# A new instruction order for a hybrid decoder layer, one sum for half of the first scale, and a last norm sum on VectorE

## The chip, the core and the metric

The kernel runs on one core of one Trainium2 chip. The metric is device time in microseconds (us) of one execution; the lower the better. A core has five engines that run side by side, each through its own list of instructions in order: PE (TensorE: matmuls), ACT (ScalarE), DVE (VectorE), POOL (GpSimd), and SP (SyncE), which here only issues DMA transfers. An instruction that has to wait for another engine or for a transfer holds up all that stand behind it on its own engine.

## The reference

One decoder layer on `x` of 1024 tokens by 1024 columns in fp32, with a vector `c` that gives shifts, scales and gates:

```python
c_act = silu(c)
mod = c_act @ w_mod + b_mod
sh1, sc1, g1, sh2, sc2, g2 = split(mod, 6)
h = rms_norm(x, norm_mix_w) * (1.0 + sc1) + sh1
proj = h @ w_in
...
h_lru = rg_lru(xr, r_pre, i_pre, lam)
out_lru = rms_norm(h_lru * gelu(y_lru), lru_norm_w)
...
out_gdn = rms_norm(o, gdn_norm_w) * silu(z)
x = x + g1 * (concatenate([out_lru, out_gdn]) @ w_out)
h = rms_norm(x, norm_mlp_w) * (1.0 + sc2) + sh2
x = x + g2 * (square(relu(h @ w_up)) @ w_down)
return rms_norm(x, final_norm_w)
```

`rg_lru` is a recurrent group of 512 channels: two gates from small block matmuls and sigmoids, then a scan over the tokens, h = a * h + b. `o` comes from the gated delta rule over four heads of 128, in chunks. The norm of `out_lru` is over all 512 channels of a token.

## The kernel before

**Numbers.** A matmul of fp32 quality is made of three matmuls on parts: each operand is split into a high part (`h`, rounded to the faster type fp32r by a cast on ACT) and a low part (`l`, the difference, on DVE or POOL), and `mm3` adds high x high, high x low and low x high in one PSUM bank. Small matmuls that need no such split (sums over partitions against `ones`, transposes) are plain fp32, each in two passes on PE. So behind nearly every matmul stand a load, a cast and a subtraction.

**Stages, in order.** (1) The start: `x` is loaded in eight tiles (`x0` to `x7`), each row is normed, transposed on PE, and scaled by A1 = (1 + sc1) * norm weight into `hT` (parts `hh`, `hl`). sc1 is a product of the vector `c_act` with a 1024x1024 part of `w_mod`. Its first 256 columns come from `scale0` (L755), one 128-column piece each, and its next 256 from `scale1(1)`, by matmuls against `cz`. The last 512 come from `scale1(2)` (L766): the weights `sc1_w20` to `sc1_w23` (512 KB each) are multiplied by `c_act` and added up over the eight row blocks k, and PE sums over partitions against `ones` (the fp32 matmuls `sc_c<-ones,sc_acc`, one per 128 columns). Before, there are two such sums, for k = 0 to 3 and k = 4 to 7; PE adds them, eight matmuls in all. Key weights `wk0` to `wk3` are loaded meanwhile, `wk0` in halves; `splitk` (L712) makes `wkh` and `wkl`, and the first matmuls are those of the four key heads (`k_p`). (2) The other projections, the delta rule's chunk inverse and its four heads' chain (`ch`, `cho`), with ACT's and DVE's steps between the matmuls. (3) The recurrent group, `lru` (L1229), four tiles of 128 channels (ct = 0 to 3). Each tile has its gates by a group of six fp32r matmuls on 64 of the 128 partitions each (`gate`), tanh on ACT (`ta`, `ti`), an exponential (`aa`), a square, a square root, then on DVE the product with the scan (`xr`) and with gelu(y) (`ly_st`). `ly_st` is stored to DRAM (`lrud`), ACT squares it (`lsq`), and L1265 adds the square to `msum` on POOL, for tiles 1 to 3 (tile 0's square is `msum` itself). (4) `rows8` (L1307) makes the norm: PE sums `msum` over partitions (`lrus`), DVE transposes, POOL takes the power -0.5 (`rsqrt8`, L529), and the row goes by DRAM (`lnd`) to be read back on all partitions (`lrus_b`). `catload` (L1333) loads `ly_st` back (`lcm0` to `lcm3`), multiplies it by `lrus_b` on DVE, and `hsplit` (L1327) makes `lch` and `lcl`. (5) The output projection: weights `wo0` to `wo7` (`wout`, L1344: parts `woh` on ACT, `wol` on DVE). The delta rule's half, `wg` (parts `gch`, `gcl` of the loaded `gcm`), can run before the recurrent norm is there. `wl` needs it (`finish`, L1394); four of its sixteen sums begin with the matmuls of `gch`. `gated` (L1374) adds the residual: `x <- wg,g,xT` on DVE, with the residual loaded as eight tiles `xT` (`residual`, L1366). (6) The second norm, once for each half of the tokens (`norm2`, L1414): `n2` sums on PE, POOL's power (`n_r`), and a transpose on PE (`n2b`). (7) The MLP: up-projection in sixteen blocks and down-projection, both by a scheme with seven products in place of eight (operands `U`, `wu`, `upx`, `upy`, `upz`; left operands `L` and right operands `R`, sums `dn`). Product at = 5 has as its right operands R0_5 to R7_5, and at = 7 R0_7 to R7_7: two loads each, a subtraction on POOL (`right`, L1673), a cast on ACT and a subtraction on DVE. (8) Residual, final norm, output tiles `fin`.

**What sets the order.** Nothing runs in the order of the source. Every instruction is recorded, and `emit` (L320 to L333) issues the records in the order of a list of numbers, `ORDER`, unpacked from the packed text `_ORDER` (L115 and on). It is a permutation of the 8013 records. `_SLOTS` says, for each tile, which buffer of its pool it gets: 46 buffers of 4 KB per partition (and 6 late ones), 8 PSUM banks. So the tables set for each engine what stands behind what; for SP they set in which order the transfers are issued, and which earlier user a load has to wait for. Nearly all DMAs are issued by SP. For that reason nearly all rows of the profile carry L333, the line that issues a record (or L459, that of a group of matmuls), and are told apart by their tiles; numbers at the end of a tile's name are left out in the profile.

Of the kernel before, what the change touches and what calls it, by code (L numbers as in the profile page):

```python
# [106 lines left out]
def dram_box(ap):  # L107
# [12 lines left out]
    'cuBSW<*M>pV)hgv~a=|gSHZ*}B7yt+XjF!lp&CO7mhb0x}Y9U^nMGb1w<B03R{s!q|W5+|4OKz@#0V4S0@CEBAVg>~c$E!R4cP0XAfA5`M5#`3KeX0!~lGn77@9ee)L'  # L120
    '^!Tx!e8@_SR5o|)XnhN>R%68L+8NB$BYrjIE-Sc4%*SbNX@V!Fv)1CA>!?r2I7u`cZ78aP&Pl0Zu3`Hm)-y%EVs){SQ`XvIrjW7rnx4nLcsaoTft<u|h6ouM%~g5zaV'
    'f=`7UI8)(olcVn=(s#XbWQTq<LtKOu@&kbOmc`tKUn4PGF>79;tDBeqP#YE3U{Sz11BnCR?$&x%YJ|`B-yE7Z9J0XeZ(M2l^OZKEayaV3k8zUp47Wymx~~H&YbZR2<A'
    'aDI4*`6dfj&bw%*3t&BfXII{wjy)Uog`4rCXWIYAs7&&rOUzAEg$POdwKm3=Q0Uk+%-4?H;#i}SGbWfuB{I#T)rn(H<@9R&*CzgLnnorM*i@$0Yj<4ic9Hab>HAddTB'
    'ja?eyd-@hp9F67n_5sa%bSe<K;tEeQEy^}kzaI)`91PBpJMPq6n;!$=78&5u7>^_aVJOb>SP_y%I=XjpGXhJsl=JmKGWUb9$5P<YfyaytDFzc=?*;8&lLI}tkhOBn@{'
    'vZ$sk=hdfar0Waa1}nJu?$Hq%zKJi4wEqu2BPPz~!h*4c9w6y4DywuD({bI5dgS+8-ln*3>>F%jKtzr?PW8FdEvd(2ie>#dmjvcZ-!O=OF9(|P78eb+u=w%U^BJytke'
    'T;7$H59|r;6>N)~1R*2A$&Y&3zHjE5Qg)11kzv6qdn?k_gych8)jTczY+yQ?d6DOW6OsM+(voLs$-=Jkk$uSw*I$T5ioT@H%o_VP*bD1mdq;DcN%*(7W|ayiR(=Po7P'
    'fm^7swZOm(~kju^*YMktFSGzObu;Q<0-VCc9pL4XsLf&190YI)co|D({*bVE>5TmfE^gp3<pyi1}WwM0RUDYkW#Z=%;!IRLqr+tqG1q*2p^BGl(Z9%e9?00PB}zdT_@'
# [1667 lines left out]
```

## Time and profile before

| | |
|---|---|
| median of 3 runs | 1124.39 us (1122.68, 1124.39, 1125.86) |
| the profiled execution | 1122.68 us, of which its span is 1120.9 |
| busy: PE / DVE / ACT / POOL | 98% / 73% / 54% / 20% of the span |
| granted clock of PE | 0.998 |
| DMA | 256.96 MB, 229 GB/s over the span |
| matmuls on PE | 6146 |

A row of the timeline has a start (us from the start of the span), a duration, the engine, the line, the operation, the tile written and those read, their shapes, how many instructions were put together (x), and in brackets how long the engine stood idle before it and what it waited for. Rows of matmuls overlap: a 512-column matmul has a duration of 0.39 us, while the next starts 0.23 later. The view of waits lists, for an engine, the tile whose instruction waited, what released it, and us in total, times, and the longest. The chain that ended last goes back from the last instruction to whatever released each step.

### The profile page before, as it was taken

The numbers are of one execution on the slowest core, as the hardware profiler recorded it, in microseconds if no ns is written. First come the engines' busy times: TensorE is split into PE (matmuls) and PEld (weight loads), VectorE is DVE, ScalarE is ACT, GpSimd is POOL, SyncE is SP. The second block draws the span as 40 slices with busy tenths as digits, with TensorE's granted clock in tenths as the row PEclk, the third lists the DMA queues.
The fourth block names the chain that finished last, engine by engine and source line by source line (L and its number), as shares of the span: only waits on it lengthen the run. The fifth ranks groups of instructions, "written<-read, shape, count | busy, mean of one in ns | idle before, by whom it ended". The sixth has DMA issues, their size and how long they took to land.

```text
span 1120.9 us, 16319 instructions
## 1 busy us (share of the span) xinstructions
PE 1099.6 (98%) x6146; PEld 916.6 (82%) x6146; DVE 822.6 (73%) x1116; ACT 603.4 (54%) x919; POOL 228.2 (20%) x149
## 2 busy tenths in 40 slices
...
GB/s 339 304 120 276 169 131 228 159 240 230 301 282 86 187 174 99 145 137 19 254 293 317 286 312 310 260 296 304 382 320 346 372 272 221 341 167 283 57 38 113
DMA packets 167785, 256.96 MB, mean 229 GB/s; under 512 B 44485, under 2 KB 88986, under 8 KB 167706
## 3 DMA queue, kind: packets, MB, share of 16 engines
...
q10 hardware_dynamic: 240, 0.23, 0.1%
...
## 4 chain that ended last, share of the span: by engine, by line
PE 56%; ACT 4%; DVE 4%; DMA 2%; issue 2%; POOL 1%; POOLq 0%; SPq 0%; DVEq 0%; ACTq 0%
PE dn L333 25%; PE upx L333 15%; PE upz L333 8%; PE wl L333 4%; PE upy L333 4%; DMA L<-aod 1%; ACT ta L333 1%; DVE xr L333 1%; ACT L333 1%; POOL R L333 1%; ACT ti L333 1%; DMA lrus_b<-lnd 1%; DVE as L333 0%; DMA lrud<-ly_st 0%; DVE U L333 0%
## 5 line engine op out<-in xcount | busy, mean ns | idle before, releaser
L333 PE MATMUL upx<-h2h,U 128*128 128x512 f32 x512 | 166.0, 394 | 0.0
L333 PEld LDWEIGHTS upx<-h2h,U 128*128 128x128 f32 x512 | 96.0, 188 | 22.9 <-ACT ek L333 0.5
L333 ACT CAST U<-wu 128x512 fp32r<-128x512 f32 x112 | 67.5, 617 | 61.6 <-DMA wu<-in_w_up_dram 7.7
L333 DVE TENSOR_TENSOR U<-wu,U 128x512 fp32r<-128x512 f32 x112 | 84.1, 766 | 19.7 <-ACT U L333 19.4
L333 POOL TENSOR_TENSOR wd<-wd,wd 128x512 f32<-128x512 f32 x32 | 46.8, 1465 | 237.0 <-DMA wd<-in_w_down_dram 154.9
L333 PE MATMUL upx<-h2l,U 128*128 128x512 f32 x256 | 91.1, 394 | 0.0
L333 PE MATMUL upz<-h2h,U 128*128 128x512 f32 x256 | 90.2, 396 | 0.2 <-DVE act L333 0.2
L333 ACT ACTIVATE act<-act 128x512 f32<-128x512 f32 x112 | 68.8, 630 | 20.2 <-DVE act L333 19.2
L333 PEld LDWEIGHTS upz<-h2h,U 128*128 128x128 f32 x256 | 47.9, 188 | 12.9 <-DVE act L333 0.8
L333 PEld LDWEIGHTS upx<-h2l,U 128*128 128x128 f32 x256 | 48.1, 188 | 11.2
L333 ACT COPY ek<-upx 128x512 f32<-128x512 f32 x48 | 28.1, 586 | 42.6 <-PE upx L333 42.1
L333 PE MATMUL upz<-h2l,U 128*128 128x512 f32 x128 | 47.7, 394 | 0.0
L333 DVE TENSOR_TENSOR act<-upz,ek 128x512 f32<-128x512 f32 x32 | 22.0, 689 | 33.4 <-PE upz L333 27.4
L333 PE MATMUL upy<-h2h,U 128*128 128x512 f32 x128 | 45.9, 396 | 0.0
L333 POOL TENSOR_TENSOR R<-R,R_5o 128x1024 f32<-128x1024 f32 x8 | 21.1, 2644 | 86.4 <-DMA R_5o<-in_w_down_dram 75.7
L333 DVE TENSOR_TENSOR wu<-wu,wu 128x512 f32<-128x512 f32 x48 | 34.8, 732 | 1.7 <-DMA wu<-in_w_up_dram 1.5
L333 ACT ACT_TABLE_LOAD x26 | 33.4, 1283 | 2.6 <-issue 2.1
L333 ACT ACTIVATE vn<-ch,bcoef 128x128 f32<-128x128 f32 x32 | 11.8, 367 | 39.0 <-PE ch L333 39.0
L333 PE MATMUL q_p<-hh,q_wh 128*128 128x512 f32 (+2 forms) x96 | 30.1, 335 | 0.0
L333 PE MATMUL q_p<-hl,q_wh 128*128 128x512 f32 (+2 forms) x96 | 29.9, 336 | 0.0
L333 PE MATMUL v_p<-hh,v_wl 128*128 128x256 f32 (+2 forms) x96 | 29.6, 333 | 0.0
L333 PE MATMUL v_p<-hh,v_wh 128*128 128x512 f32 (+2 forms) x96 | 29.4, 333 | 0.0
...
## 6 DMA issues: line engine op xcount, KB each, us to landing
L<-aod SPq DMA_DIRECT2D x56, 512.0 KB, 5.8
R<-in_w_down_dram SPq DMA_DIRECT2D x40, 512.0 KB, 7.4
wu<-in_w_up_dram SPq DMA_DIRECT2D x32, 512.0 KB, 5.5
...
wd<-in_w_down_dram SPq DMA_DIRECT2D x32, 512.0 KB, 5.0
...
sc_w<-in_w_mod_dram SPq DMA_DIRECT2D x16, 512.0 KB, 8.8
sh_w<-in_w_mod_dram SPq DMA_DIRECT2D x16, 512.0 KB, 5.8
```

What stands on the lines that cost most here:

```text
L333: op.fn(*[res(v) for v in op.a], **{n: res(v) for n, v in op.k.items()})
```

## The change

Three things.

1. `scale1(2)` keeps one sum over the eight row blocks in place of two over four each. ACT's first multiplication is done once, not twice; DVE has seven steps of multiply and add, not six; PE sums the result by four matmuls with start and stop, not by eight that add up in pairs.
2. The addition of the last tile's square to `msum` (ct = 3) is done on DVE. Tiles 1 and 2 stay on POOL.
3. `_ORDER` and `_SLOTS` are other tables: 8009 records (four PE steps less) in another order, and other buffers.

```diff
 _ORDER = (
-    'c-noN2b5Js@aC)Uo4^3W5Qm&4OOzleS#kyuB!eUo2`VBvC<1~35W$3jq<|zv$%rDLg5)e2B<C;;^Iq5fx(D6=p0m4fVBXx&U0wCnS6}tLuc)Mz-5M?CzrT;m12q!xDO'
...
+    'c-oDdcbJq#v-YcJHn1#9PLi|aC^-rW2qGv*P!LcMkRU2aB*+VjWD!J?<RBRVL2?dC&RLR3PD@ypo#{HiZg}5w&Ohh-uDy14=b7i}P<7W`cXjs^kmM3Ae`ur_|5HdJ<*'
...
-        for a in range(0 if q == 2 else 2, 2):
-            acc = big(f"sc1_acc{q}{a}")[:, 0:w]
-            for k in range(4):
-                wt, c = sc1_w[q, (4 * a + k) // m][:, (4 * a + k) % m, :], cact[:, 4 * a + k:4 * a + k + 1]
+        if q == 2:
+            acc = big(f"sc1_acc{q}")[:, 0:w]
+            for k in range(NK):
+                wt, c = sc1_w[q, k // m][:, k % m, :], cact[:, k:k + 1]
                 if k == 0:
                     A.mul(acc, wt, c)
                 else:
                     V.scalar_tensor_tensor(out=acc, in0=wt, scalar=c, in1=acc, op0=ALU.mult, op1=ALU.add)
             for j in range(n):
-                mm(pc[:, j:j + 1], acc[:, j * P:(j + 1) * P], ones[:, 0:1], a == 0 and j == 0, a == 1, skip_group_check=True)
+                mm(pc[:, j:j + 1], acc[:, j * P:(j + 1) * P], ones[:, 0:1])
...
-            G.tensor_tensor(out=msum, in0=msum, in1=sq, op=ALU.add)
+            (V if ct == 3 else G).tensor_tensor(out=msum, in0=msum, in1=sq, op=ALU.add)
```

Unpacked and matched record by record, the two orders differ as follows where the prediction looks:

- SP's queue at the start, before: x0, x2, x1, sc1_w00, x3, wk0 (first half), sc1_w01, sc1_w10, sc1_w11, wk0 (second half), wk1, sc1_w20, sc1_w22, sc1_w21, x4, sc1_w23, wk2, x7, wk3. After: x0, x3, x1, x2, sc1_w00, sc1_w20, wk0 (first half), sc1_w21, sc1_w01, sc1_w22, sc1_w23, wk0 (second half), sc1_w10, sc1_w11, x4, wk1, wk2, x6, x5, wk3.
- The residual's loads `xT` stand earlier in SP's queue. Around the recurrent norm SP had lcm2, the store of the last `ly_st`, lnd, lcm0, lrus_b, three loads of wu and lcm3. Now it has lcm0, the store of the `ly_st` before the last, lnd, the load of wo3, the store of the last `ly_st`, lrus_b, and then lcm3 and lcm2.
- On PE, `lrus` and the first `wl` that reads `lch` had 48 instructions between them, and have 63. The first `gate` stands earlier by 1.0 us of PE work.
- On ACT, wo3h leaves the stretch ahead of the last square and wo2h comes into it.
- On DVE, the low part of R6_5 stands right behind that of R4_5, no longer behind those of R7_5 and L0_7. On POOL, R7_7 stands ahead of R6_7.
- Between `n2` and `n2b` PE has 3.1 us of other matmuls each time, where it had 1.5 and 1.7.

"PE work" of a place in the list is the sum of the usual spacings of the matmuls ahead of it, as the trace of before has them.

More of the change, by code (lines that the diff above doesn't have):

```diff
@@ L120 @@
[L120 to L127, printed above, removed]
@@ new lines @@
+    '6DuswE|c|6*jn=HU8eHS&M`l#%nAPgZMv{*RMQ|Lg9;a+3Ewg7Kj}T2W@|2-&RXwTvv+r`kg1X+U1)uCP{+xZsA+Q;n6faztN|zqOVGWiQVj;`gflqo0WCL>(tlGS!c'
+    '`NFc%*f5(6qeZ8Tt@mfpP>Z`I<3(8VW&?3yRu59#UY9zmEH$T2({2j-yk>*-WLbSI{D@kR!r#tmMxubEszoB*HCigDYS@hgof9KPK`b?8aX-4l_n;5Y=sgCw!^y9exx'
+    'h!Hf%5MY7p%Wyhl$2yVeOXt^w|>N1^a@XZ!zhw7i&fYoLekJ%lpNPjCBJ;3-^*vZho_SCfsLRotA}NZ9?^z!LVGZ;WBLY98hKT+$P=r&Q1W2kqEd=yzK$4@^iWgrR7j'
+    '`jczs9e$YT9lPia#bs~<@!X(OY#dO;6qT3T2^>(%9v2C>jXRc)mE@kK1p@6tcCqx8`?rHf3%Pe<|2CTubf-yPNraz*pt$wrccUe9V#jpwfcFOke=5VPtfD|zY`*6%6L'
@@ new lines @@
+    'bgeGZ+5BCi?ZjcrNIA32zK(Yn>ujAWqx4HG7$xZ?QSa(0djfw2xbho5&n_+Gu&rgf@oX&p_16xxkz2mznTI++zmZG&u}<QXOSJV~Fgjd_>&rD-8Z(x`v{PBrncFrqp4'
+    '=2@Z13BGky(>MdN7bLoECpJq}^*+JKpZqmU4?xzNEJ#vtGf<J2VBaUG=!$m1qr`kWG+ZGzxq~nCn_kw_~?o@OE`QBHv&|s|R>3DZAvBrqP>tHeORpEq$!z{u2#Hv?jJ'
+    'HF12YntlhB1P*8Cmyc=1EwIXGwF5~JlnXKFO39Y;To8qaUJi)%p7;6juI+Q)qb&NOYBQ}cHrn*cV%0lW8a#$ni=d$Jo$vd&fRvpOuZCX{{C9>*CU!4~yV+-<0Uzx6>e'
+    'TzvRzr}gFuW4o7l|uh3&VL47o%COlP7=WJAt_4lU*csWDH%<2o`0n28IzF?W}M9;9hl=bFt%PF>Ua42c`KuJwGMzMo?_oSMC$Xaw{?jLN_$&2(3p39!bV1gdjz)8))U'
@@ new lines @@
+    '%vb}03qaeS(0^+Ua3(#R%T%~(y;*X-NDE#ZDz#zfF(C2+dLR+si>o0gYJwz%n_@mfGuVugM7qOK=;3TeH-XuDWjgWwtRq5dcb>=&k#PLUNhom4eT?P_|OPxRH6d-j~{'
+    '!H-q(T`w7c{fEgK?Wp6KSz1P(Qs!%Oe7X(nr|@I#$KAV$=P<~-%m1mQznNq!niiT_nrT@^*$l>9BfabhbKkrd&ZE&rttFD<<OD5*@W^DFB@mER_OY!bd*w5ePSR;>JJ'
+    'Bq#%>w=HD4Af-NHhAX$PC{%U2H9h3N+H6Y+B;zfDFecyR~+(Oejt|npIqNmb+rZjJR%KgsmbsZ5zX!1BWz^Zj#gCE`i^)p7aP02}}*A546;?a@R)5EZfnnwAll%;;YQ'
+    'M6vl050@$Uf{%+qeujz7lWGHAFBDIMKL)5s4U#@S<Ang4JyUYi@ky0KDKEkVU0V8>}oB3E5*}<|<cj#1;Q6B62b_fx3N@m(Q<^#J~%IGf8ydGYPgKhguH9g3+>L7Ow_'
```

224 lines of the change are left out of this document (110 added, 114 removed).

## The prediction

> **What bounds the kernel.** I read the page first, then who waited for whom on PE, then the busy time by stages, then the chain that ended last.
>
> ```profile
> span 1120.9 us, 16319 instructions
> PE 1099.6 (98%) x6146; PEld 916.6 (82%) x6146; DVE 822.6 (73%) x1116; ACT 603.4 (54%) x919; POOL 228.2 (20%) x149
> ```
> ```profile
> PE wl L333 <- ACT lch L333: 3.5, 1, 3.5
> PE wg L333 <- DVE x L333: 2.2, 1, 2.2
> PE dn L333 <- DVE R_5l L333: 2.1, 1, 2.1
> PE n2b L333 <- POOL n_r L333: 1.6, 2, 0.9
> PE ch L333 <- DVE nv L333: 1.5, 1, 1.5
> ...
> PE iw L459 <- ACT LT L333: 1.0, 1, 1.0
> PE gate L459 <- ACT ly_st L333: 0.7, 1, 0.7
> PE lrus L459 <- POOL msum L333: 0.6, 1, 0.6
> ```
>
> PE is busy for 98% of the span. Its named waits (us in total, times, longest) are few: the eight above add up to 13.2 us, and no clock column below is under 1.00. A new order can win hardly more than those, and only matmuls that vanish come on top. So the question is which of these waits go, and which new ones come.
>
> ```profile
> 0.00:30.00 30.00, 28.96 (x235) 26.25 (x235) 16.34 (x43) 18.32 (x29) 5.23 (x14) 1.00 0.99 332
> ...
> 346.00:385.00 39.00, 39.00 (x247) 34.69 (x246) 26.41 (x24) 35.95 (x42) 8.41 (x5) 1.00 0.46 154
> 385.00:412.00 27.00, 24.06 (x104) 17.63 (x102) 21.83 (x21) 21.04 (x27) 4.00 (x2) 1.00 0.85 202
> 412.00:428.20 16.20, 12.08 (x57) 8.98 (x56) 8.87 (x12) 1.60 (x3) 3.49 (x3) 1.00 0.62 197
> ```
>
> Busy time by stretch, for PE, PEld, DVE, ACT and POOL, then the clock, the DMA share and GB/s. Between 346 and 385 ACT works 35.95 of 39 us, and from 385 to 428.2 PE stands for 2.9 and 4.1 us. That is the recurrent group: its gates, its scan, and the norm that all four of its tiles must share. There ACT and the norm, not PE, set when `wl` can go on. Everywhere else PE sets the time.
>
> **The recurrent norm.** Its chain, from the view of the chain that ended last, with rows of POOL, DVE and PE between:
>
> ```profile
> 382.10 1.04 ACT wo3h L333
> ...
> 409.60 4.71 DMA lrud<-ly_st
> ...
> 417.52 1.60 DMA lnd<-lrus_w
> ...
> 419.17 6.86 DMA lrus_b<-lnd
> 426.12 1.24 DVE lcm L333
> 427.45 0.63 ACT lch L333
> 428.12 6.98 PE wl L333 x28
> ```
> ```profile
> 410.39 2.40 POOL L333 TENSOR_TENSOR msum<-msum,lsq 128x1024 f32<-128x1024 f32 x1 [7.83 <-ACT lsq L333]
> ```
> ```profile
> 405.61 0.62 ACT L333 CAST U<-wu 128x512 fp32r<-128x512 f32 x1 [0.88 <-DVE xr L333]
> ```
> ```profile
> 407.93 1.23 DVE L333 TENSOR_TENSOR ly_st<-ly_st,xr 128x1024 f32<-128x1024 f32 x1
> 409.07 0.68 DVE L333 TENSOR_TENSOR gcl<-gcm,gch 128x512 fp32r<-128x512 f32 x1
> ...
> 410.63 0.75 DVE L333 SCALAR_TENSOR_TENSOR x<-wg,g,xT 128x512 f32<-128x512 f32 x1 [0.21 <-PE wg L333]
> ```
> ```profile
> 412.84 0.64 PE L459 MATMUL lrus<-msum,ones 128*32 128x256 f32 x8 [0.62 <-POOL msum L333]
> 413.41 0.50 PE L333 MATMUL wg<-gch,wo5l 128*128 128x512 f32 x1
> 413.75 0.39 PE L333 MATMUL wg<-gcl,wo4h 128*128 128x512 f32 x1
> 413.98 0.39 PE L333 MATMUL wg<-gch,wo6l 128*128 128x512 f32 x1
> ...
> 428.12 0.96 PE L333 MATMUL wl<-lch,wo0h 128*128 128x512 f32 x3 [3.50 <-ACT lch L333]
> ```
>
> From `lrus` at 412.84 to the first `wl` at 428.12 the chain takes 15.3 us. Starts of 512-column matmuls lie 0.23 apart (413.75, 413.98). The decoded lists have 48 PE instructions from `lrus` to that `wl` before, some 11.5 us, and 63 after: 15 more, 15 x 0.23 = 3.5 us. That fills the 3.50 us of wait, but PE gains by it only what `wl` itself starts sooner, since these matmuls are taken from ahead of `lrus`. So I follow `wl`'s start.
>
> It has three parts. First, the last msum moves to DVE. An addition of 128x1024 took 2.40 on POOL and 1.23 on DVE (row 407.93), so -1.2. In the new list gcl and one x (0.68, 0.75) stand ahead of it on DVE, but both can be done while ACT squares; I take -1.0, with ends -1.2 and +0.4 (the 1.43 of the two, if they come late). Behind it on DVE are only x updates and PE's next bank has room. Second, ACT: of its 101 operations from the first gate's to the last square wo3h (1.04) and a cast of U (0.62) leave, and wo2h, of wo3h's size, comes in. As ACT is nearly full there, -0.6, ends -1.2 and +1.2 (one cast of this size more or less on the chain). The wait of `wg` (2.2) doesn't count by itself: it lies beside this chain, and PE will now stand ahead of `lrus` instead. Third, when the stage begins, which hangs on the start of the kernel.
>
> **One sum for half the scale, and the loads of the start.**
>
> ```profile
> 19.16 1.05 ACT L333 CAST wkh<-wk 128x1024 fp32r<-128x1024 f32 x1 [1.25 <-DVE wkl L333]
> ```
> ```profile
> 23.30 2.85 DVE L333 SCALAR_TENSOR_TENSOR sc_acc<-sc_w,cact,sc_acc 128x512 f32<-128x512 f32 x4
> ```
> ```profile
> 23.69 0.62 PE L333 MATMUL k_p<-hh,wkh 128*128 128x512 f32 x2
> ...
> 27.85 1.17 PE L333 MATMUL sc_c<-ones,sc_acc 128*128 128x1 f32 x10
> ```
> ```profile
> sc_w<-in_w_mod_dram SPq DMA_DIRECT2D x16, 512.0 KB, 8.8
> ```
>
> One sum in place of two takes one ACT multiplication away, adds one DVE step (2.85 / 4 = 0.71), and takes four fp32 sums off PE, eight passes of 0.12 (1.17 / 10): -0.9 on PE, early on. Against that stands where the new list puts it: its four loads of 512 KB and its seven DVE steps (5.0 us) come ahead of the second half of the first key weight. On SP's queue wk1 had x0 to x3, both halves of wk0, sc1_w0 and sc1_w1 ahead of it; now it has sc1_w2 (4 x 512 KB) and x4 as well, 2.6 MB more. The first stretch moves 332 GB/s at a DMA share of 0.99, so wk1 lands 2.6 / 0.332 = 7.9 us later. Before, it had landed by 19.16, when ACT cast it, and PE first used it at 23.69. In the new list its first use comes 0.36 us of PE work later, at 24.05. Cast at 19.16 + 7.9 = 27.1 at the latest, 1.05 for the cast: 28.1, so at most 4.0 us lost; at the least none, if it had landed long before 19.16. By the bytes ahead of it it landed about a microsecond earlier: I take -2.9 us, that is, PE is 2.9 late.
>
> What gives some of that back before the gates: the first gate stands 1.0 us of PE work earlier in the list (by the same count; the eight passes are most of it), and up to it the list has 18 fewer changes between fp32 and fp32r matmuls (341 for 359). One costs PE 0.11: after `lrus` the next start comes 0.34 later (413.41 to 413.75) in place of 0.23. 18 x 0.11 = 2.0. So the stage begins 2.9 - 1.0 - 2.0 = -0.1, about as before; ends -3.0 (nothing lost at the start) and +3.0 (4.0 lost, changes without effect). `wl` starts at 0 - 1.0 - 0.6 = -1.6.
>
> After it: the list holds 0.7 us less PE work behind the first `wl`, since some is placed ahead of it: -0.7.
>
> **The loads of that stage.** The residual's loads (xT, eight) go out sooner, but x was late only for `wg`. SP now has, behind lnd, wo3, the store of the last ly_st, lrus_b, lcm3, lcm2. So lrus_b has 1 MB ahead of it, where it had lcm0's 0.5 MB; 1.6 us of it are covered by lnd's own landing. At the 0.332 MB a us of the first stretch half a MB is 1.6 us, of which I take half, +0.7, ends -1.5 (the 6.86 of lrus_b was long for its size) and +1.6.
>
> ```profile
> lcm<-lrud SPq DMA_DIRECT2D x4, 512.0 KB, 8.6
> ```
>
> lcm3 reads what that store wrote, and lcm2 stands behind it in the queue. lnd goes out at 417.5 - 1.6 = 415.9, the store a microsecond later, landing 4.7 after that at 421.6; lcm3 and lcm2 then land 8.6 later, at 430.2 and 430.6. With DVE's 1.24 each and ACT's 0.63 they are ready at 432.1 and 433.4, later by any x update (0.75) that DVE has ahead of them. By the count `wl` wants lcm2 6.9 us after its first matmul and lcm3 8.3 after: 428.1 - 0.9 + 6.9 = 434.1 and 435.5. The cover is under 1 us, where lcm2 had 3: I take +0.6, ends 0 and +3.5, the row of `wl`.
>
> **The two later waits.** n2b waits 1.6 in all, for POOL's power between two PE steps. The new list puts 1.5 us more work between the two each time (3.1 in place of 1.5 and 1.7): -1.6. `dn`:
>
> ```profile
> 948.10 2.31 DVE L333 TENSOR_TENSOR R_5l<-R,R_5h 128x1024 fp32r<-128x1024 f32 x1
> ...
> 966.71 3.40 DVE L333 TENSOR_TENSOR R_5l<-R,R_5h 128x1024 fp32r<-128x1024 f32 x1
> ```
> ```profile
> 970.17 0.50 PE L333 MATMUL dn<-R_5l,L_5h 128*128 128x512 f32 x1 [2.14 <-DVE R_5l L333]
> ```
>
> The step that PE waits for (966.71) stands on DVE behind R7_5's and L0_7's, whose inputs came late; the new list puts it right after the one at 948.10, so it ends some 16 us sooner: -2.1. On POOL, R7_7 and R6_7 change places and R6_7's low part is wanted 8.4 us sooner; it has more than that, +0.3.
>
> PE's list is otherwise another one: of its 5285 recorded steps, 1954 at most stand in the same sequence in both. Waits of the kind of `ch`, `iw` and `gate` (1.5 + 1.0 + 0.7 = 3.2) may go or come; ends 0 and +3.2, and I take a third, +1.0.
>
> **The sum:** -1.6 + 0.7 + 0.6 - 0.7 - 1.6 - 2.1 + 0.3 + 1.0 = -3.4. The profiled execution took 1122.68, 1.8 more than its span, and is the fastest of three; it becomes 1119.3. The median of 1124.39 becomes 1121.0. The tail after the last matmul stays.
>
> **Rivals.** *The stall only moves* (chance 0.23). Up to its last square the stage hangs on ACT, with 35.95 of 39 us busy. If the 4.0 at the start comes whole and fewer changes of type give nothing, the gates begin 3.0 late: -3.4 + 3.1 = -0.3, 1124.1. For it: PE's waits ahead of `wl` then sit at `lrus`. Against it: the gates stand earlier in the list.
>
> *SP's queue makes it slower* (0.18). Loads put back in the queue come late for their steps: wk1 at the start, then lcm3 and lcm2 behind the late store. Price: the start 3.1 over my sum, lcm2 2.9 over it, 3.5 as in the row of `wl`, and lrus_b 0.9 over it: -3.4 + 6.9 = +3.5, 1127.9; with 2.2 more of unknown waits 1130. It decides once wk1's cast ends after 28 and lcm2 lands after 433. For it: a DMA share of 0.99 in the first stretch, and 0.85 just ahead of lcm2.
>
> *More is won* (0.13). wk1 was early enough, and lrus_b lands 1.5 sooner: -3.4 - 2.9 - 2.2 = -8.5, 1115.9.
>
> *The clock falls at the start* (0.03). Row first: after 3.50 of wait `wl` went on with three starts within 0.96, and the clock column stays at 1.00. If a wait of 3 us at wk1 halved the clock for as long, 1.5 would be added: -1.9, 1122.5. The Trainium skill, "TensorE: Matmul & The Clock Gate", in the section "What's actually happening", says that PE falls to half its clock after an idle window of some 3.4 us and needs as much busy time to come back, which speaks against an order that lets PE stand at the start; the row at 428.12, at the edge of that window, shows no such fall.
>
> *The forecast* (0.43): 1118.0 to 1124.0, around 1121.0.
>
> **The numbers.** A measurement of this kernel can tell some 0.3%, 3.4 us: faster is below 1121.0, slower above 1127.8. Of the forecast 0.29 lies below 1121.0, a little more than half, since 1.6 of its sum are waits that no row shows; with the larger gain's 0.13, and 0.05 of the moved stall and the clock, faster 0.47. Slower: 0.16 of the queue's 0.18 and 0.02 of the moved stall, 0.18. Same: the remaining 0.35. The range, by the ends of the terms and the rivals, leaves out the far half of the larger gain and the worse part of the queue's case: 1115.0 to 1128.3.
>
> **What would show it.** Right: a row `lrus <- DVE msum` and `lrus` near 411.2; `wl` at about 427.2 with under 1 us of wait; no rows of n2b and of dn <- R_5l; the first 128x512 k_p near 27. Wrong: k_p beyond 28, a wait of `wl` for lcm2 or lcm3 over 1, a wait of gate over 2 us, or new rows of dn that add up to more than 2.

## The result and the profile after

| | before | after |
|---|---|---|
| median | 1124.09 us (1122.68 to 1125.86, 4 runs) | 1137.74 us (1136.11 to 1140.30, 4 runs) |
| ratio, 95% interval | | 1.0123 [1.0099, 1.0147] |
| profiled span | 1120.9 us | 1136.1 us |

The change costs 13.7 us; the prediction was 1121.0, with 1128.3 as the upper end. The first lines of the page of the kernel after, and its view of PE's waits (us in total, times, longest):

```profile
span 1136.1 us, 16284 instructions
PE 1107.8 (98%) x6138; PEld 918.1 (81%) x6138; DVE 830.8 (73%) x1118; ACT 596.0 (52%) x916; POOL 227.7 (20%) x148
```
```profile
PE gate L459 <- ACT lx_st L333: 3.6, 1, 3.6
PE q_p L333 <- ACT z_st L333: 2.2, 1, 2.2
PE k_p L333 <- ACT wkh L333: 1.8, 2, 1.1
PE lrus L459 <- DVE msum L333: 1.8, 1, 1.8
PE upx L333 <- DVE U L333: 1.4, 2, 0.8
...
PE ch L333 <- DVE r L333: 1.2, 1, 1.2
...
PE dn L333 <- DVE R_6l L333: 1.0, 1, 1.0
PE upz L333 <- DVE U L333: 1.0, 1, 1.0
PE wg L333 <- ACT gch L333: 1.0, 1, 1.0
```

The rows of `wl`, `n2b` and `dn <- R_5l` are gone, as forecast. In their place stand `gate` for `lx_st`, `q_p`, `k_p`, `upx`, `upz`, `wg` for `gch`, a second `ch` and `R_6l`, none of which the view of before had (its only `gate` waited 0.7, for `ly_st`). PE has 8 instructions fewer and is busy 8.2 us longer: it was slower at the same work. The view of busy time by stretch, for two of the stretches that the prediction used (the last three columns are the clock, the DMA share and GB/s), says where:

```profile
0.00:30.00 30.00, 26.18 (x208) 22.59 (x209) 15.28 (x44) 16.33 (x28) 5.22 (x15) 0.94 0.98 347
346.00:385.00 39.00, 35.39 (x220) 29.88 (x219) 28.30 (x31) 33.02 (x42) 15.81 (x6) 0.96 0.31 109
```

The clock column is at 0.94 and 0.96 in two stretches that had 1.00 before. Cut finer, the clock falls to half for stretches of 3.41 us, and all of them begin on one grid, that is, whole multiples of 3.41 us apart. Below are three of the five falls of the kernel after, each with the stretch ahead of it. Behind the comma, the first number is the time that PE was busy in the stretch; the clock is the third from the end.

```profile
131.35:134.76 3.41, 1.34 (x10) 1.02 (x8) 3.17 (x10) 1.66 (x3) 0.00 (x0) 1.00 1.02 401
134.76:138.18 3.41, 3.26 (x12) 2.97 (x13) 3.17 (x8) 3.38 (x6) 0.00 (x0) 0.50 0.88 331
...
377.11:380.52 3.41, 0.00 (x1) 0.00 (x0) 1.44 (x3) 2.00 (x4) 0.68 (x2) 1.00 0.68 268
380.52:383.94 3.41, 3.22 (x13) 2.20 (x14) 0.17 (x1) 2.85 (x5) 1.91 (x1) 0.50 0.05 12
680.90:684.31 3.41, 1.85 (x8) 0.90 (x7) 3.24 (x2) 2.41 (x5) 3.26 (x3) 1.00 0.89 305
684.31:687.72 3.41, 3.41 (x9) 2.65 (x10) 0.22 (x1) 0.00 (x0) 0.97 (x1) 0.50 0.65 184
```

Here a stretch in which PE stood for about half its length or more is followed by one at half clock. That costs up to 3.41 / 2 = 1.7 us of PE work. The kernel after has five ahead of its last matmul (at 22, 135, 230, 381 and 684 us); the profile of before has one, at 170. Not all of them fit the half: ahead of the fall at 22 PE was busy for 2.30 of 3.41 us, and ahead of before's own at 170 for 2.43, with small matmuls. Nor is one fall usual for the kernel before: in the 28 executions beside e13 to e16 its mean clock lay between 0.990 (1129.6 us) and 0.998 (1121.1 us), and the profile shown is among the best. The 3.50 us of wait ahead of `wl` before brought none, and the same cut shows why:

```profile
423.00:426.41 3.41, 1.62 (x8) 0.97 (x6) 0.29 (x1) 0.00 (x0) 0.00 (x0) 1.00 0.85 303
426.41:429.83 3.42, 1.71 (x7) 1.38 (x8) 3.42 (x5) 2.38 (x5) 1.60 (x2) 1.00 0.98 338
```

The wait lies across a border of the grid, so that each half still had PE busy for 1.6 to 1.7 us. In e1 below, which has the same order but for the engine of one addition, `wl` waited 3.1 us inside one stretch (PE busy for 1.05), and two stretches at half clock followed.

To see where the rest came in, I took for each matmul its start less the PE work ahead of it in the list (the prediction's "PE work"), and call it PE's lateness. A rise is lost time, whatever its cause; the small matmuls that some experiments add are lost time too. Each row is one execution, the profiled one.

| lateness (us) at PE work of | 20 | 120 | 230 | 310 | 340 | 400 | 460 | 670 | 890 us | the end |
|---|---|---|---|---|---|---|---|---|---|---|
| before | 5.9 | 8.4 | 19.3 | 25.2 | 25.4 | 34.9 | 37.5 | 38.1 | 38.4 | 40.8 |
| after | 10.9 | 16.0 | 30.7 | 37.3 | 42.8 | 47.0 | 47.4 | 53.4 | 56.6 | 56.5 |
| e7: after, waits filled | 9.8 | 14.5 | 26.8 | 33.4 | 37.6 | 42.6 | 43.1 | 47.3 | 49.1 | 49.0 |
| e16: three waits mended, rest filled | 10.3 | 12.5 | 25.6 | 32.1 | 35.1 | 39.9 | 40.4 | 45.4 | 45.9 | 46.3 |
| e9: new order up to 310, then the old one | 10.8 | 16.0 | 30.8 | 37.3 | 42.7 | 54.4 | 57.0 | 60.2 | 60.1 | 64.0 |
| e15: old order, middle part new and mended, filled | 6.0 | 8.6 | 18.1 | 24.5 | 30.7 | 35.6 | 37.0 | 38.1 | 38.0 | 37.9 |

After is 5.0 behind at the start, 12.1 at the recurrent group (310), 17.4 behind its third gates (340), 9.9 once the recurrent norm is through (460: here the new order gains 7.5), then 15.3 in the MLP's up-projection (670), 18.2 at 890, and 15.7 at the end. Between 120 and 230 it loses 3.8 more than before; the waits that the view lists there add up to only 1.3 more (3.8 against 2.5), and each kernel has one fall there, so that most of this loss stays open. The places of the other losses, by their rows. First the gates at 381 us, from the timeline of after:

```profile
380.72 0.80 PE L459 MATMUL gate<-xrh,gw 64*128 64x512 f32 x2 [3.61 <-ACT lx_st L333]
```
```profile
371.74 1.22 DVE L333 TENSOR_TENSOR zz<-zz,on_b 128x1024 f32<-128x1024 f32 x1
372.87 2.28 DVE L333 TENSOR_TENSOR_SCAN xr<-aa,xr 128x1024 f32<-128x1024 f32 x1
375.19 3.23 DVE L333 TENSOR_TENSOR ly_st<-ly_st,xr 128x1024 f32<-128x1024 f32 x1
378.34 0.15 DVE L333 COPY ly_b<-ly_p 128x1 f32<-128x1 f32 x1
378.41 0.14 DVE L333 COPY lx_b<-lx_p 128x1 f32<-128x1 f32 x1
```
```profile
378.52 0.47 ACT L333 ACTIVATE ly_st<-ly_p,ly_b 128x256 f32<-128x256 f32 x1 [3.72 <-DVE ly_b L333]
378.89 1.05 ACT L333 ACTIVATE lsq<-ly_st 128x1024 f32<-128x1024 f32 x1
379.84 1.41 ACT L333 ACTIVATE lx_st<-lx_p,lx_b 128x256 f32<-128x256 f32 x3
```
```profile
373.08 4.25 POOL L333 TENSOR_TENSOR xrl<-xr,xrh 128x1024 fp32r<-128x1024 f32 x1 [4.80 <-DVE zz L333]
```

PE wants a bank that ACT's `lx_st` empties; ACT wants `ly_b` and `lx_b`, two copies of 0.15 us, which stand on DVE behind a scan and a product; and the product takes 3.23 instead of 1.22 (same shape, row above) beside POOL's `xrl`. By the Trainium skill, page "SBUF — State Buffer", section "SBUF: two separate sides", VectorE with two SBUF inputs and GpSimd lock each other out of one shared port for a whole instruction; this trace agrees, the one being 2.0 us longer here. `xrl` itself, which began during the scan, takes 4.25 where one at 317.76 took 2.39. The same at 684 us:

```profile
676.83 0.69 DVE L333 TENSOR_TENSOR U<-wu,U 128x512 fp32r<-128x512 f32 x1
...
680.67 3.47 DVE L333 TENSOR_TENSOR U<-wu,U 128x512 fp32r<-128x512 f32 x2
```
```profile
680.27 1.64 POOL L333 TENSOR_TENSOR wd<-wd,wd 128x512 f32<-128x512 f32 x1 [14.03 <-DVE act L333]
681.98 1.61 POOL L333 TENSOR_TENSOR wd<-wd 128x512 f32<-128x512 f32 x1
```
```profile
682.50 0.51 PE L333 MATMUL upx<-h2h,U 128*128 128x512 f32 x1 [0.60 <-DVE U L333]
...
684.20 0.71 PE L333 MATMUL upz<-h2h,U 128*128 128x512 f32 x1 [0.96 <-DVE U L333]
684.70 0.63 PE L333 MATMUL upx<-h2l,U 128*128 128x512 f32 x1
685.13 0.63 PE L333 MATMUL upz<-h2l,U 128*128 128x512 f32 x1
```

Two sums of U take 3.47 together where one before them took 0.69, PE waits 0.60 and 0.96, and then runs at 0.43 from start to start (684.70, 685.13), half its pace: waits of 1.6 us were followed by a fall of the clock that can cost as much again (1.7). `q_p` and the start:

```profile
132.88 0.15 DVE L333 COPY z_b<-z_p 128x1 f32<-128x1 f32 x1
```
```profile
134.92 0.58 PE L333 MATMUL q_p<-hh,q_wh 128*128 128x256 f32 x1 [2.22 <-ACT z_st L333]
```
```profile
14.33 0.39 PE L333 MATMUL k_p<-hh,wkh 128*128 128x256 f32 x1 [0.67 <-ACT wkh L333]
17.88 0.38 PE L333 MATMUL sc_c<-ones,sc_row 128*128 128x1 f32 x2 [0.95 <-DVE sc_row L333]
20.41 0.39 PE L333 MATMUL k_p<-hh,wkh 128*128 128x256 f32 x1 [1.11 <-ACT wkh L333]
...
29.39 0.60 PE L333 MATMUL k_p<-hh,wkh 128*128 128x512 f32 x2
```
```profile
15.11 2.32 DVE L333 SCALAR_TENSOR_TENSOR sc_acc<-sc_w,cact,sc_acc 128x512 f32<-128x512 f32 x3
17.53 0.29 DVE L333 COPY sc_row<-sc_r 128x128 f32<-128x128 f32 x1
```

`z_b`, another copy of 0.15, stands in the middle of the inverse's long chain on DVE. At the start three steps of the one sum stand on DVE ahead of the copy `sc_row` that PE waits for. PE's result `sc_c` then gives the scale that ACT's next `hh` needs, and behind `hh` on ACT stands the cast `wkh` for which PE waits 1.11.

### The profile page after: what moved, and what is told of

It is laid out like the page before. It is cut to its first block, busy times and chain, and to the rows that moved or that the text cites. A ratio compares the mean times of both kernels' runs of the same rounds, so it can differ in the third digit from the quotient of the medians.

```text
span 1136.1 us, 16284 instructions
## 1 busy us (share of the span) xinstructions
PE 1107.8 (98%) x6138; PEld 918.1 (81%) x6138; DVE 830.8 (73%) x1118; ACT 596.0 (52%) x916; POOL 227.7 (20%) x148
## 4 chain that ended last, share of the span: by engine, by line
PE 57%; DVE 4%; ACT 3%; issue 1%; DMA 1%; POOLq 0%; POOL 0%; DVEq 0%; ACTq 0%
PE dn L333 27%; PE upx L333 14%; PE upz L333 7%; PE wl L333 5%; PE upy L333 4%; PE wg L333 1%; DVE U L333 1%; ACT ta L333 1%; DVE as L333 1%; DMA wd<-in_w_down_dram 0%; ACT act L333 0%; ACT L333 0%; ACT ti L333 0%; DVE ta L333 0%; DVE xr L333 0%
## 5 line engine op out<-in xcount | busy, mean ns | idle before, releaser
L333 PE MATMUL upx<-h2h,U 128*128 128x512 f32 x512 | 168.6, 395 | 1.4 <-DVE U L333 1.4
L333 PE MATMUL upx<-h2l,U 128*128 128x512 f32 x256 | 93.8, 397 | 0.0
L333 PE MATMUL upz<-h2l,U 128*128 128x512 f32 x128 | 47.4, 397 | 0.0
L333 DVE TENSOR_TENSOR wu<-wu,wu 128x512 f32<-128x512 f32 x48 | 37.4, 790 | 0.7 <-DMA wu<-in_w_up_dram 0.6
L333 ACT ACT_TABLE_LOAD x24 | 30.8, 1283 | 10.7 <-DVE c L333 7.7
L333 PE MATMUL v_p<-hl,v_wh 128*128 128x258 f32 (+2 forms) x96 | 30.1, 341 | 0.0
L333 PE MATMUL v_p<-hh,v_wh 128*128 128x256 f32 (+2 forms) x96 | 30.1, 338 | 0.0
L333 PE MATMUL v_p<-hh,v_wl 128*128 128x258 f32 (+2 forms) x96 | 29.6, 336 | 0.0
```

The source lines that it names most:

```text
L333: op.fn(*[res(v) for v in op.a], **{n: res(v) for n, v in op.k.items()})
```

## The experiments

Two theories to begin with: that the start's loss is carried through to the end, and that single waits of the new order, each with a fall of the clock behind it, make the rest. The rivals are that waits only move, and that falls of the clock come by chance and cost nothing that an order could save. Ratios are to the kernel before, run on the same chip beside each experiment, with 95% intervals. Where an edit changes the tables, its diff is given in words.

**e1, the last msum on VectorE alone.**

```diff
-            G.tensor_tensor(out=msum, in0=msum, in1=sq, op=ALU.add)
+            (V if ct == 3 else G).tensor_tensor(out=msum, in0=msum, in1=sq, op=ALU.add)
```

> The kernel before, in its old order, with one edit: the last addition to msum on DVE. Theory A (the new order is to blame, the three edits of the arithmetic are not): the addition falls from 2.40 to about 1.25 and lrus, lnd, lrus_b and the first wl come 1.0 to 1.2 sooner, so 1123 against 1124.1, a change of -0.5 to -1.2. Theory B (the edit itself hurts, since DVE has x updates queued and PE's banks wait for them): +0.5 to +2, with a wait of wg.

1124.75 us, 0.9992 [0.9971, 1.0012]: nothing that can be told from no change. The prediction's -1.0 is within the interval, and not shown.

**e2, one sum for half the scale alone**, in the order before.

```diff
...
-            acc = big(f"sc1_acc{q}{a}")[:, 0:w]
...
+            acc = big(f"sc1_acc{q}")[:, 0:w]
...
```

> The kernel before, in its old order, with one edit: one sum over the eight row blocks for the second half of sc1. Theory A: eight passes of 0.12 go from PE, the last sum is ready one DVE step later, and the start is otherwise as before: -0.3 to -1.0, so about 1123.5. Theory B (the longer sum delays the second half of hT): the key matmuls on those rows wait for it, +0.5 to +2.

1131.05 us, 1.0050 [1.0028, 1.0071]: slower by 5.6 us, beyond both theories. This part, worth -0.9 of PE work, costs more than it saves in the old order. Its row of PE's waits:

```profile
PE sc_c L332 <- DVE sc_acc L332: 2.8, 1, 2.8
```

The seven steps now follow each other on VectorE, the last two behind `rs`, a step of x4's norm that waits for ScalarE, and PE stands 2.8 us for the last; a fall of the clock follows at 32 us. Its profile has falls at 408, 431 and 974 us besides; that of e1, in the order before, has such at 170, 426 and 973.

**e18, the same with the sum's last two steps ahead of the step that waits for x4.**

```diff
 VectorE's queue
-sc_acc (5 steps), rs, sc_acc (2 steps)
+sc_acc (7 steps), rs
```

> The run e2 again (the order before, one sum for half the scale), with the sum's last two steps on VectorE ahead of the step of x4's norm (rs), which waits for ScalarE. Theory (the one sum cost 5.6 us in e2 only by its place: 2.8 us of wait at sc_c for its last step, and a fall of the clock behind it): the wait shrinks below 1.5 us and no fall follows, 3 to 6 us less than e2's ratio of 1.005: 0.9997 to 1.0023. Rival (seven steps in a row on VectorE are later than two sums side by side wherever they stand): 1.004 to 1.006.

1129.16 us, 1.0034 [1.0018, 1.0051]. The wait shrinks from 2.8 to 1.7, above what the theory said, and the fall, at 31 us, stays. The measured ratio lies between the two ranges. Place is part of it, but here too the seven steps in a row, 5.47 us in its trace, end at 28.7, where the two sums' last ended at 27.7 (26.91 + 0.75).

**e4, the new start in the old order** (first 350 records of the new order, both other parts of the change too), and **e3, the old start in the new order** (with the one sum).

```diff
 e4
-ORDER = before
+ORDER = after[:350] + the rest in before's order
 e3
-ORDER = after
+ORDER = before[:350] + the rest in after's order
```

> The other way round: the kernel before with the first 350 records in the new order (and one sum, and the last msum on DVE). Theory A (carried): +4 to +5 against the kernel before, less about 1 for the other edits, so 1127 to 1129. Theory C (taken up by the recurrent group's waits, 9 us of them between 365 and 428): within 1.5 of the kernel before. What I forecast at first was 2.9 at the start, 2.0 of it given back.

> The changed kernel with the first 350 records (through about 36 us) in the old order, all the rest in the new. The offset of PE against its work is 10.9 after the start in the changed kernel and 6.25 before, 4.6 more, with one fall of the granted clock in it. Theory A (what is lost at the start is carried to the end): 4 to 5 less than the changed kernel, about 1133. Theory B (the late start also sets off the later waits of q_p and ch and their falls of the clock): 7 to 10 less, 1128 to 1131. Theory C (it is taken up again by waits further on): less than 1.5 gained.

e4: 1132.08 us, 1.0074 [1.0053, 1.0094]. Its lateness is 15.0 at 60 us of PE work against 6.8 before, and 49.2 at the end against 40.8: 8.2 us lost at the start, 8.4 at the end. Nothing behind it takes any of it back. This is more than the theory had, and not the changed kernel's own start: that one stands at 11.3 at 60, so that 3.7 of the 8.2 belong to e4 alone, whose clock falls for two stretches where the changed kernel's falls for one. e3: 1142.69 us, 1.0156 [1.0121, 1.0192], no faster than the changed kernel. The old start with one sum waits as in e2 (2.9 at `sc_c`, and a fall of two stretches behind it), and its lateness at 60 us is 15.9. So e3 says nothing on the new start itself.

**e10, the old start with both sums in the new order**, to mend e3.

```diff
-before[:350] with one sum
+before[:350] with both sums
```

> The kernel before for its first 350 records, with both sums of the scale's half, and the changed kernel's order from there on. Theory (the new start's 4.6 us are carried to the end by TensorE, which is busy 98% of the time): 4 to 5 us less than the changed kernel's 1137.7, 1132.7 to 1133.7, and the waits at q_p, gate200, upx and dn stay as they were. Rival (the later stages wait for VectorE, ScalarE and GpSimd, whose work does not come sooner): the waits there grow by what the start saves, 1136 to 1138.

1135.49 us, 1.0114 [1.0086, 1.0142]: 4 to 5 us less was expected, 1 to 2 came (by the ratios or by the medians), within the intervals of both. Where the two orders join, PE waits three times more (0.58 and 0.63 for `ab`, 1.09 for `sh_r`), and lateness at 60 is 10.0, hardly below the 11.3 of after. The waits at `q_p` and `gate` stay as they are (lateness steps of 2.3 and 3.8): they don't hang on how late PE comes. Inconclusive on the start.

**e9, the new order up to 310 us of PE work, then the old one.**

```diff
-ORDER = before
+ORDER = after[:gates of tile 2] + the rest in before's order
```

> The changed kernel's order up to 310 us of TensorE's work, and the order before from there on. Theory (what the first part loses, 12 us in the profile with its three falls of the clock, is carried to the end, since TensorE is the bound engine): 1133 to 1137. Rival (the waits for wg, wl and n2b behind it are set by ScalarE, VectorE and GpSimd and shrink by as much as TensorE comes later): 1124 to 1128.

1144.51 us, 1.0165 [1.0137, 1.0193]. The rival (late operands absorb it) is out: lateness is 12.1 above before at 310 and never comes nearer than that. It is more than the theory had: the old rest now brings four falls of the clock of its own (357, 421, 445, 991 us) and a longer wait at a gate. `wl` waits nearly as long as before, 3.3 for 3.5.

**e6, the clock by itself.** 512-column matmuls in runs of 40 to 53, with gaps made by VectorE.

```diff
+run(60)
+for i, wd in enumerate(_GAPS):
+    gap(wd)
+    run(_RUNS[i % 3])
```

> Leaves out all of the layer and writes zeros: runs of 40, 47 or 53 matmuls of 512 columns with gaps between them that are made by VectorE, three of each length from some 0.5 us to 6 us, then short runs of 2 to 15 matmuls between gaps of one length, to measure when the granted clock falls. Theory A (any gap over a bound is followed by half the clock): the falls start at one length, and all longer gaps have them. Theory B (it goes by the phase of the gap against fixed time windows of the clock's control): gaps of one length have the fall in some repeats and not in others, the more often the longer the gap, and short runs between short gaps bring it too.

The run without the layer took 945.83 us. Between its long runs, waits of up to 1.70 us were never followed by a fall, of 2.20 in one of three, of 2.51 in two of three, of 2.94 and more in all. That is as theory B says. Two pairs of stretches on the grid, both around a wait of 2.20:

```profile
241.72:245.14 3.42, 1.46 (x6) 1.24 (x7) 1.84 (x3) 0.00 (x0) 0.00 (x0) 1.00 0.00 0
245.14:248.55 3.41, 3.41 (x9) 2.63 (x9) 0.00 (x0) 0.00 (x0) 0.00 (x0) 0.50 0.00 0
255.38:258.79 3.41, 1.78 (x8) 1.47 (x9) 1.51 (x3) 0.00 (x0) 0.00 (x0) 1.00 0.00 0
258.79:262.20 3.41, 3.41 (x16) 2.77 (x15) 0.00 (x0) 0.00 (x0) 0.00 (x0) 1.00 0.00 0
```

The same wait of 2.20 brings the fall where it lies in one stretch (PE busy 1.46) and not where a border cuts it (1.78). Over the whole run, 25 stretches at full clock had PE busy for at most 0.43 of them, and all 25 were followed by half clock; of the 206 with 0.45 or more, one was. Runs of five matmuls between waits of 0.97 us brought it too, runs of ten didn't: short waits add up inside a stretch. The Trainium skill, "TensorE: Matmul & The Clock Gate", section "What's actually happening", has the free-running window of 3413 ns, which the grid here agrees with, and the fall after an idle window, which it doesn't: a window a little over half idle was enough.

**e7, the changed kernel with its waits filled.** 43 small matmuls add zero to open sums ahead of seven waits.

```diff
+nc.tensor.matmul(b.get()[0:64, 0:128], zf.real(), ones.real(), start=False, stop=False, skip_group_check=True)
```

> The changed kernel with 43 small matmuls of zeros (64x128, adding zero to sums that are open anyway) ahead of seven waits: at sc_c (5) and k_p (5) at the start, q_p (8), ch1_0 (5), gate200 (13), upx10 (3) and upz8 (4). They take some 60 to 70% of each wait and nothing else. Theory (the half clock that follows these waits costs about 1.7 us each time, and it follows since TensorE stood still): the five falls of the changed kernel go, 6 to 8 us less than 1137.7: 1129.7 to 1131.7. Rival (the falls come whatever is run in the waits, or come elsewhere instead): 0 to 1.5 us less, 1136.2 to 1137.7, with as many windows under 0.9 of the clock.

1131.85 us, 1.0085 [1.0059, 1.0112]; no stretch at half clock before the last matmul, and a mean clock of 0.999 for 0.990. Over before it is 8.5 us slower by the medians, the changed kernel 13.7: its falls were worth some 5.2 us (4.3 by the ratios, whose intervals are some 3 us to either side), a little under the 6 to 8 expected, with the late operands themselves untouched. The rival is out.

**e5, the two copies ahead of the scan and the product; e12, `lx_st` ahead too.**

```diff
 VectorE's queue
-xr1 (scan), ly1_st, ly2_b, lx3_b
+ly2_b, xr1 (scan), lx3_b, ly1_st
 ScalarE's queue, e5
-ly2_st, lsq1, lx3_st (3), xr3
+ly2_st, lx3_st (3), xr3, lsq1
 ScalarE's queue, e12
+lx3_st (3), xr3, ly2_st, lsq1
```

> The changed kernel, with VectorE's two copies that feed the third and fourth sub-head's gates (lx_b and ly_b) put ahead of the scan xr1 and of the product ly1_st, and with ScalarE's square lsq1 put behind xr3. Theory (the 3.6 us wait for lx_st ahead of gate200 and the clock's fall behind it come of the order on VectorE and ScalarE): the wait goes below 1 us, no fall at 380 us, 3.5 to 5 us less than the changed kernel's 1137.7: 1132.7 to 1134.2. Rival (the norm's sums behind it set the end of this stage anyway, so that the wait turns up at lrus or at wl): 0 to 1.5 us less, 1136.2 to 1137.7.

> The changed kernel with the copies ly_b and lx_b ahead of the scan and of the product on VectorE, as in the run e5, and beyond that with ScalarE's three lx_st and xr3 ahead of ly_st, so that nothing in front of gate200 waits for the product ly1_st. Theory: gate200 waits under 0.5 us and no fall follows at 380 us, 3.5 to 5 us less than the changed kernel: 1132.7 to 1134.2. Rival (the wait comes back at ly2_p1, at lrus or at wl): 1136 to 1138.

e5: 1140.31 us, 1.0144 [1.0109, 1.0180], no gain, and neither theory: the wait stayed where it was (a step of lateness of 4.2 at `gate200`). With the copies done at 375.6 and 377.8, ACT still stood:

```profile
381.12 1.28 ACT L332 ACT_TABLE_LOAD   x1 [5.06 <-DVE ly_st L332]
```

ACT's next result, `ly2_st`, has its place in SBUF where `xr1` was, and that is free only once the product `ly1_st` has read it. A second edge behind the one that the profile named. e12 goes around it: no wait at `gate200` and no fall at 380 us in its profile, but 1.94 of wait at the next group of gates, for the same `ly_st`; 1137.41 us, 1.0101 [1.0070, 1.0132]. The median lies in the rival's range, the ratio 2.5 us below the change's, with intervals that overlap: a gain at the gates isn't shown, and the wait moved for the greater part.

**e8, the new order between 310 and 450 us only; e11, the same with e12's order and R6_5l ahead of L0_7l.**

```diff
 e8
-ORDER = before
+ORDER = before up to 310, after's up to 450, before's
 e11, VectorE's queue, besides e12's
-L0_7l, R6_5l
+R6_5l, L0_7l
```

> The kernel before up to the gates of the third sub-head (TensorE's work up to 310 us) and again from wl's last quarter on (450 us), and between the two the changed kernel's order; both sums of the scale's half, msum's last sum on VectorE. Theory (the three parts add up, and the middle part alone is worth what the profile of the changed kernel gains there, 12.3 us of waits against 10.1): 1 to 3 us less than before, 1121 to 1123. Rival (the middle gains nothing by itself, since its gate200 waits 3.6 us and brings a fall of the clock for what wl no longer waits): 1124 to 1127.

> The same middle part, with VectorE's copies ly_b and lx_b ahead of the scan and of the product ly1_st, ScalarE's three lx_st ahead of ly_st (whose place in SBUF is freed only by that product) and of lsq1, and in the last part R6_5l ahead of L0_7l on VectorE. Theory (the wait at gate200 was made by the order of those two queues; R6_5l's wait of 2.3 us by L0_7l ahead of it): 6 to 9 us less than before, 1115 to 1118. Rival (what gate200 gains is waited for at lrus or wl, and dn51 waits for the next operand): 1120 to 1123.

e8: 1126.15 us, 1.0014 [0.9999, 1.0028]: the rival holds, the part that wins at `wl`, `wg` and `n2b` loses as much at its gates. e11: 1122.17 us, 0.9979 [0.9968, 0.9991]: faster than before, by 2.9 us by the medians, but in the rival's range. `dn51`, the sum that waited for R_5l, waits no more; the gates wait 4.2 in two groups, for `ly_st`, and the profile has three falls of the clock (344, 375, 420 us).

**e13, three waits mended in the changed kernel; e16, the same with the rest filled.**

```diff
 VectorE's queue, besides e12's
-ftmp, xx (18 steps), z2_b
+z2_b, ftmp, xx (18 steps)
-as7 (3 sums), act8, wu9, U10_6
+U10_6, as7 (3 sums), act8, wu9
```

> The changed kernel with three of its new waits mended at their places: VectorE's copy z_b ahead of the inverse's chain of ftmp and xx (for q_p), the lx_st order of the run e12 (for gate200), and the sum U10_6 ahead of as7's sums on VectorE (for upx10). Theory (each of these waits is made by one instruction's place on VectorE, and each brings a fall of the clock of 1.7 us): q_p and upx10 stop waiting, 6 to 10 us less than the changed kernel's 1137.7, 1128 to 1132. Rival (TensorE finds the next late operand a few us on): 1135 to 1138.

> The same with 35 small matmuls of zeros ahead of the waits that are left (sc_c, k_p, ch1_0, upx10, upz8, gate251, lrus). Theory (what is left over the kernel before is then the longer wait at the start, some 3.5 us, and the chain's waits, some 3 us, less 5 us that the middle and last part gain; the falls are gone): 1123 to 1128. Rival (falls were not worth 1.7 us each): within 1.5 us of the run without the small matmuls.

e13: 1132.64 us, 1.0058 [1.0035, 1.0081], 7.3 us less than the change by the ratios, inside the theory's 6 to 10 (the median just above its 1132). `z_st` holds `q_p` up no longer, `upx` waits 0.6 for 1.4, `gate` 1.9 for 3.6, now for `ly_st`. That each wait mended takes its fall along isn't borne out: the profile of e13 has five stretches at half clock ahead of its last matmul and a mean of 0.990, both as the changed kernel's. Those at 135 and 684 are gone, one at 379, by the gates, is still there, and two are new, a second at the start and one at 424. As e12, which mends the gates alone, has 2.5 of the 7.3, and that within its interval, the better part lies at `q_p` and `upx`. e16: 1128.53 us, 1.0025 [1.0008, 1.0042]. So of the change's 1.0123 (13.8 us) the three places together were 7.3 us, filling the rest 3.7, and 2.8 are left; 6.3 against the kernel before without its falls (e14, below).

**e17, e16 with the sum's steps moved off the start's chain.**

```diff
 VectorE's queue
-sc_acc (3), sc_row, sc_acc, A, sc_acc, A, sc_acc (2), hl
+sc_acc (2), sc_row, sc_acc, A, A, sc_acc (2), hl, wkl, sc_acc, hl, sc_acc
```

> The kernel of the run e16 (three waits mended, small matmuls of zeros in the others) with the start changed too: VectorE's copy sc_row and its two steps of A no longer stand behind three and five steps of the one sum, but between them; ScalarE's cast of the second half of wk0 ahead of hh, which waits for A; TensorE's four sums over sc_acc some 1.5 us of its work later. Theory (the waits of 0.95 at sc_c and 1.11 at k_p come of the one sum's seven VectorE steps, which stand ahead of what the first keys need): those two waits shrink to under 0.5 us together, 1 to 2 us less than e16 (1128.5, ratio 1.0025). Rival (the start is bound by its loads, at a DMA share of 0.98): within 0.7 us of e16, with the wait at wkh of the next weight instead.

1130.76 us, 1.0053 [1.0033, 1.0072]: slower than e16 by the ratios, with intervals that overlap, and not the gain of the theory. The trace shows a faulty test: the small matmuls of e16 still stood ahead of `sc_c` (1.31 us) and now ended a microsecond after the operand was there, and ACT's `hh` waited for its place in SBUF until a step of the sum had read it:

```profile
21.04 0.84 ACT L333 ACTIVATE hh<-xTq,A 128x256 fp32r<-128x256 f32 x2 [2.10 <-DVE sc_acc L333]
```

The cast of wk0's second half, now ahead of `hh`, began at 18.33, when its load had landed; in the changed kernel it began at 19.74. By that, the load leaves some 1.4 us to be won at that place (an estimate across two executions); what makes the rest of the start's loss stays open between the sum's place and its buffers.

**e14, the kernel before with its own waits filled; e15, e11 filled.**

```diff
 small matmuls, by the matmul that waits behind them
+e14: ch1_0 5, wg11 8, wl20 13, dn51 8
+e15: ch1_0 5, gate151 8, gate251 8, wg11 4, lrus 7
```

> The kernel before, its order untouched, with 34 small matmuls of zeros ahead of its own waits at ch1_0 (5), wg11 (8), wl20 (13) and dn51 (8). Theory (a wait that leaves TensorE idle for over half of one fixed stretch of 3.4 us of the clock's control halves the clock for the next; the waits of the kernel before lie near that bound, so that some executions have such falls and others not, as the profile with one and the others with two to four show): 1 to 3 us less than before in the median, 1121 to 1123.5. Rival (falls come by chance, whatever TensorE does): 1123.5 to 1126.

> The kernel of the run e11 (the old order with the changed one's middle, mended) with 32 small matmuls of zeros ahead of its waits at ch1_0 (5), gate151 (8), gate251 (8), wg11 (4) and lrus (7). Theory (its profile had three falls before the end, at 344, 375 and 420 us, 1.7 us each): 2 to 5 us less than e11's 1122.2, 1117 to 1120. Rival: 1121.5 to 1123.5.

e14: 1122.25 us (1120.73 to 1125.08, 10 runs), 0.9979 [0.9962, 0.9995], where the kernel before had 1124.78 (1120.99 to 1129.58, 28 runs). Matmuls that compute nothing make it faster by 2.5 us and narrow its spread: the theory holds. With the waits of both filled (e7 against e14) the change still costs 11.0 us by the medians, 11.9 by the ratios: its falls, net of those that the kernel before has, are 2 to 3 of the 13.7 us, and the rest is PE's late operands and what stays open. e15: 1120.52 us (1119.03 to 1121.87, 8 runs), 0.9961 [0.9943, 0.9978], no fall ahead of the last matmul, 1.7 below e11 where 2 to 5 were expected. It is faster than both kernels, by 4.3 us than before; 2.5 of these the filling gives alone (e14). The intervals of e14 and e15 overlap, so the middle part's own share isn't settled by them.

## Why the prediction was wrong

**"Waits of the kind of `ch`, `iw` and `gate` ... may go or come; ends 0 and +3.2, and I take a third, +1.0."** This is the step that failed most. The waits that no row of before showed (gate 3.6, q_p 2.2, upx 1.4, ch for r 1.2, dn for R_6l, upz and wg for gch 1.0 each) come to 11.4. The bound was taken from what the old order happened to leave. But at least 3331 of PE's 5285 steps stand in another sequence, and those of ACT and DVE were shuffled as well; a copy of 0.15 us behind a scan and a product then costs what those cost. e13 shows it for the first three together: moving one or a few instructions at each place took 7.3 us away, the better part of it at `q_p` and `upx`; at the gates a gain isn't shown.

**"The clock falls at the start" (0.03), since "the row at 428.12 ... shows no such fall".** The changed kernel's falls were worth some 5 us (e7), of which 2 to 3 are beyond what the kernel before pays in its usual execution (e14). One row without a fall was no evidence: that wait lay across a border of the grid, and in e1 the same wait brought one. The rival named only the start; four of the five falls are elsewhere, behind waits of 1.3 to 3.6 us.

**The start: 2.9 late, given back by 1.0 and by 18 x 0.11.** The 2.9 rests on wk1's load, and that is not what PE came late for. wk1's cast came at 27.78, where 27.1 had been put as the latest, but it stands on ACT behind an `hh` that waited for the scale from PE:

```profile
wk<-in_w_in_dram SPq DMA_DIRECT2D x3, 512.0 KB, 7.1
```
```profile
26.63 1.27 ACT L333 ACTIVATE hh<-xTp,A 128x512 fp32r<-128x512 f32 x2 [1.04 <-PE sc_c L333]
27.78 1.05 ACT L333 CAST wkh<-wk 128x1024 fp32r<-128x1024 f32 x1
```

The load went out at 14.93; with the median of 7.1 us to landing, wk1 was there at about 22 (an estimate), over 5 us ahead of its cast. PE was late by then, through the waits for `sc_row` (0.95) and for wk0's second half (1.11), both behind the sum's steps on DVE, and through the fall at 22. The first 128x512 `k_p` came at 29.39, beyond the 28 set as wrong, and without a wait of its own. Lateness is 5.0 over before at 20 us, not 2.9, and nothing of it came back: 12.1 at 310. No run isolates the 2.0 put on fewer changes of type. e4 shows a start's loss carried whole. That the sum is one was priced as a gain of PE work and not as seven DVE steps in a row: e2 and e18 put that at 5.6 and 3.8 us by the ratios in the old order.

**`wl` at 427.2.** It came 13.2 later, nearly all of it from what lay ahead:

```profile
425.37 0.64 PE L459 MATMUL lrus<-msum,ones 128*32 128x256 f32 x8 [1.77 <-DVE msum L333]
```
```profile
L333 PE MATMUL wl<-lch,wo0h x7: 391/394/398, 440.4 to 445.5; 128*128 128x512 f32 x7
```

The chain itself was well sized: 15.0 us from `lrus` to `wl`, 15.3 before. `wl` doesn't wait, and lcm2 and lcm3 came in time (0 for +0.6). The stage from 380 to 460 us of PE work gains 7.1 (its lateness rises from 30.0 to 37.5 before, from 47.0 to 47.4 now), more than the sum had. Part of it may come only of PE being late itself; e8 shows that the part alone gains nothing.

**n2b -1.6, dn -2.1.** Right: both rows are gone. R_6l came in with 1.0, where +0.3 had been put.

**The rivals.** *SP's queue* was the one on the slower side, at 1127.9 to 1130. Its side was right and its mechanism wasn't: wk1's cast ended after 28, but not because of its load, and lcm2 and lcm3 came in time. *The stall only moves* had its sign, a longer wait at `lrus` (1.8 for 0.6), but foresaw no loss. Nothing of *more is won* came.
